# A new order of all steps in a grouped-query attention kernel, with the first bfloat16 transfers placed among GpSimd's products

## The chip, the core and the metric

The kernel runs on one core of a Trainium2 chip. The time is device microseconds of one execution. The kernel before took 352.64 us (median of three runs, 352.6 to 353.29). The engines are named as in the profile: PE (TensorE, matmul), PEld (its weight load), DVE (VectorE), ACT (ScalarE), POOL (GpSimd), SP (SyncE, which here only issues transfers).

## What is computed

Softmax attention with 8 query heads and 2 key/value heads per batch, 8 batches, 1024 positions, head dimension 64. There are 64 heads in all, numbered over batches; heads 0 to 3 use the first k and v of batch 0, heads 4 to 7 the second, and so on.

```python
batch, n_q_heads, n_kv_heads, seq, head_dim = (8, 8, 2, 1024, 64)
scores = scale * np.matmul(q_group, k_group.transpose(0, 1, 3, 2))
scores_max = np.max(scores, axis=-1, keepdims=True)
attn = np.exp(scores - scores_max)
attn = attn / (np.sum(attn, axis=-1, keepdims=True) + 1e-08)
output[:, q_start:q_end, :, :] = np.matmul(attn, v_group)
```

## The kernel before

**Tiles.** One head has 8 score tiles. A tile is 128 key positions by 1024 query positions (two matmuls, L400) in one of three PSUM slots (`sp0` to `sp2`). A slot is free again when its tile has been read by ACT or DVE. 366 of the 512 tiles go to ACT, which exponentiates them in one instruction (L411, into `pt`). The other 146 go to DVE, which computes an approximate exponential by bit arithmetic, in these steps: L422 scales the scores into 16-bit integers (`ye`), reading PSUM; L431 takes their mantissa into `zz`; `zz` is multiplied by `ye`, partly on DVE (L457), partly on POOL (L448); L463 masks `ye` in place to its exponent. The weight of such a tile is the sum of `ye` and `zz`, so PE multiplies both by v; for the last three heads DVE adds them first (L474). L431, L463 and the products work on a chain of one or two tiles (1024 or 2048 columns), as `LENGTHS` says. The mask of a chain has to wait for every product of it, since it overwrites `ye`.

**Second product.** PE multiplies the weights by v, with a column of ones that gives the sum of the weights (L491; L529 for head 0 and the last head, whose products are made tile by tile). An output piece is 128 query positions by 65 columns. Seven pieces share a PSUM bank; then DVE takes the reciprocals (L560) and normalises (L571) into `ost`, and SP stores a head at a time (L378).

**Transfers.** q, k and v are float32 in HBM. A transfer on POOL's queue casts them to bfloat16 in a scratch tensor in HBM (`qd`, `kd`, `vd`; L174): one head or two heads of q, one or two k or v of a batch. SP then brings them in: q and k through transposing transfers (L243 into `qt`, L233 into `kt`, which L237 and L238 copy to the other half of the partitions), v by plain ones (L226 into `va`). POOL is one queue: a product behind a transfer waits for the transfer's descriptors to be written.

**Order.** Nothing is scheduled by the compiler. A string, `ORDER`, holds one letter for each step, in one sequence for all engines, and a loop in the kernel issues the steps as it reads them; each engine keeps its own part of that sequence. `A0` are the scores of the next tile for ACT in slot 0, `a` to `g` those of a tile for DVE (of the current head, the next, and so on), `x` an exponential, `p` L422, `z` L431, `G2,78` a product on POOL of 8 x 78 columns of the chain two before the newest, `m` the rest of the product on DVE, `t` the mask, `+` the sum, `V` up to four matmuls of the second product, `E` and `L` those of the first and the last head, `F` a dummy matmul, `r` and `n` reciprocal and normalisation, `S` a store, `T`, `K`, `C`, `U` the transfers on SP (q, k, k's copy, v), and `q`, `k`, `v`, `X`, `Y`, `Z` those on POOL. The capital three wait besides for the last scores matmul issued before them in the sequence:

```python
if now and gate:
    tc.add_manual_dep(ins.ins, now.ins.name, Sync, reason="loads in time, not sooner")
```

A product on POOL waits for the DVE step ahead of the last of DVE's steps that work from SBUF to SBUF:

```python
tc.add_manual_dep(gps.ins, gate.ins.name, Sync, reason="the port goes to the step behind it")
```

`ORDER` begins behind a fixed head of the program: loads of the first q, k and v, their casts and transposes on PE, and the transfers of q for heads 1 and 2.

Of the kernel before, what the change touches and what calls it, by code (L numbers as in the profile page):

```python
# [606 lines left out]
```

## Time and profile before

| | before |
|---|---|
| median of three runs | 352.64 us |
| the profiled execution | 352.72 us |
| its span, first to last instruction | 350.9 us |
| mean granted clock of PE | 0.995 |
| exponentials on ACT (L411) | 366 |
| L422 on DVE | 146 |
| products on POOL (L448) | 126 |

The profiled execution is one of its own; its span leaves out 352.72 - 350.9 = 1.82 us around the instructions. A row of a timeline gives start and duration in us, the engine, the line of the kernel, the operation, output and input, and in brackets the idle time of the engine ahead of it with what ended it. A row that groups instructions gives their count, total busy time, the mean of one in ns, and the idle time ahead of them.

### The profile page before, as it was taken

To read this page: it belongs to the slowest core of one execution; us is meant where nothing else is said; L and a number is where in the kernel's file an instruction comes from. 1 tells how busy PE (TensorE), PEld (TensorE's weight loads), DVE (VectorE), ACT (ScalarE), POOL (GpSimd) and SP (SyncE) were. 2 spreads that over 40 slices of the span, in tenths; PEclk is the share of its full clock that TensorE was granted. 3 is DMA by queue.
4 is the path that set the end of the run, shared out by engine and by line. 5 is a ranking of instruction groups with operands and counts; after the bars stand their busy time and mean duration, and the time that the engine had idled before them with its cause. 6 is when DMAs were issued, how large, how long until landed. Compare 5 with 4: busy or idle time off the path is not lost.

```text
span 350.9 us, 14187 instructions
## 1 busy us (share of the span) xinstructions
PE 340.2 (97%) x6268; PEld 225.7 (64%) x6268; DVE 342.1 (97%) x518; ACT 339.8 (97%) x370; POOL 288.6 (82%) x236
## 2 busy tenths in 40 slices
PE   7879999999999999999999999999999999999995
PEld 3446665666676666666666666666665666667774
DVE  5999999999999999999999999999999999999996
ACT  5997999999999999999999999999999999999994
POOL 3496989999988999998999989899998989987000
PEclk9998999999999999999999999999999999999999
DMA  5879577865978778666768976678778765533123
GB/s 150 123 151 178 108 152 138 137 135 95 149 147 116 154 151 131 118 131 138 147 122 112 151 156 133 119 136 158 122 136 138 116 148 98 113 83 86 48 84 102
DMA packets 96606, 44.84 MB, mean 128 GB/s; under 512 B 61184, under 2 KB 95360, under 8 KB 95744
## 3 DMA queue, kind: packets, MB, share of 16 engines
q1 hardware_dynamic: 94128, 31.34, 42.3%
q0 software_dynamic: 2128, 12.19, 24.9%
q8 instruction: 49, 0.80, 1.0%
q10 hardware_dynamic: 288, 0.39, 0.3%
q14 instruction: 13, 0.11, 0.2%
HBM read 27.13 MB, written 28.97 MB: 160 GB/s over the span
## 4 chain that ended last, share of the span: by engine, by line
PE 55%; DVE 30%; ACT 8%; issue 3%; DMA 2%; SPq 0%; DVEq 0%
PE ops L491 30%; PE sp L400 24%; DVE ye L422 15%; ACT pt L411 8%; DVE ye L463 4%; DVE zz L431 4%; DVE ost L571 3%; DVE zz L457 3%; DMA kt<-kd 2%; DVE rec L560 1%; PE ops L269 1%; PE sp L529 1%; PE sp L292 0%; DVE kt L313 0%; PE ops L304 0%
## 5 line engine op out<-in xcount | busy, mean ns | idle before, releaser
L411 ACT ACTIVATE pt<-sp 128x1024 bf16<-128x1024 f32 x366 | 337.3, 1052 | 3.4 <-PE sp L400 3.2
L448 POOL TENSOR_TENSOR zz<-ye,zz 128x568 bf16<-128x568 bf16 (+29 forms) x126 | 248.5, 1973 | 25.4 <-DVE zz L431 9.0
L422 DVE TENSOR_SCALAR ye<-sp 128x1024 uint16<-128x1024 f32 x146 | 177.1, 1213 | 1.3 <-PE sp L400 0.8
L400 PE MATMUL sp<-qt,kt 64*128 64x512 bf16 x1024 | 166.5, 383 | 4.3 <-ACT pt L411 3.0
L491 PE MATMUL ops<-va,pt 128*128 128x65 bf16 x2832 | 160.6, 194 | 0.0
L491 PEld LDWEIGHTS <-pt 128*128 128x128 bf16 x2832 | 120.5, 98 | 30.7 <-issue 30.7
L491 PE MATMUL ops<-va,zz 128*128 128x65 bf16 x1136 | 123.8, 194 | 0.0
L491 PE MATMUL ops<-va,ye 128*128 128x65 bf16 x1104 | 119.6, 194 | 1.3 <-DVE ye L463 1.3
L491 PEld LDWEIGHTS <-ye 128*128 128x128 bf16 x1104 | 83.9, 98 | 16.9 <-issue 14.8
L491 PEld LDWEIGHTS <-zz 128*128 128x128 bf16 x1136 | 86.5, 98 | 9.8 <-issue 9.5
L400 PEld LDWEIGHTS <-kt 64*128 64x128 bf16 x1024 | 51.6, 93 | 58.9 <-issue 34.9
L463 DVE TENSOR_SCALAR ye<-ye 128x2048 uint16<-128x2048 uint16 (+1 forms) x77 | 51.6, 676 | 0.0
L431 DVE TENSOR_SCALAR zz<-ye 128x2048 uint16<-128x2048 uint16 (+1 forms) x77 | 49.7, 657 | 0.1
L571 DVE TENSOR_TENSOR ost<-ops,rec 128x448 f32<-128x448 f32 (+2 forms) x73 | 44.4, 608 | 0.3
L457 DVE TENSOR_TENSOR zz<-ye,zz 128x2048 bf16<-128x2048 bf16 (+31 forms) x54 | 33.4, 622 | 0.0
L174 POOL DMA_DIRECT2D qd<-in_q_dram x34 | 23.7, 697 | 5.6 <-PE sp L400 4.6
L560 DVE RECIPROCAL rec<-ops 128x7 f32<-128x7 f32 (+2 forms) x73 | 14.1, 194 | 0.0
L443 POOL MEMSET tick<- 128x1 bf16 x52 | 9.7, 187 | 0.0
L174 POOL DMA_DIRECT2D vd<-in_v_dram x8 | 5.9, 735 | 0.0
L174 POOL DMA_DIRECT2D kd<-in_k_dram x8 | 5.7, 712 | 0.0
L269 PE MATMUL ops<-warm 128*128 128x512 bf16 (+1 forms) x12 | 3.5, 448 | 1.2 <-DVE warm L168 1.2
L529 PEld LDWEIGHTS <-pt 128*128 128x128 bf16 x96 | 3.4, 98 | 1.2 <-issue 1.2
(37 smaller groups left out, 27.2 us busy)
## 6 DMA issues: line engine op xcount, KB each, us to landing
out_dram<-ost SPq DMA_DIRECT2D x63, 256.0 KB, 3.2
qd<-in_q_dram POOLq DMA_DIRECT2D x28, 256.0 KB, 4.7
kt<-kt SPq DMA_DIRECT2D x30, 64.0 KB, 3.7
va<-vd SPq DMA_DIRECT2D x30, 64.0 KB, 3.2
kd<-in_k_dram POOLq DMA_DIRECT2D x7, 256.0 KB, 4.8
vd<-in_v_dram POOLq DMA_DIRECT2D x7, 256.0 KB, 5.3
qt<-qd SPq DMA_TRANSPOSE x63, 4.2
qd<-in_q_dram POOLq DMA_DIRECT2D x7, 128.0 KB, 3.3
```

The lines of the kernel that those rows point to most:

```text
L174: return nc.gpsimd.dma_start(out=t.rearrange("(a x) d -> a (x d)", a=128), in_=src.rearrange("(a x) d -> a (x d)", a=128),)
L400: now = nc.tensor.matmul(sps[x][:, hf, :], lhsT=t[lo : lo + D, c // NH, ci % NH * 128 : (ci % NH + 1) * 128], rhs=qt[j][lo : lo + D, 0, :] ...
L411: exps.append(nc.scalar.activation(out=p, in_=where_s[(j, c)], func=AF.Exp, scale=scale))
L422: vec = nc.vector.tensor_scalar(out=ye[:, i, :, :], in0=where_s[(j, c)], scalar1=EXP_A, scalar2=EXP_B, op0=ALU.mult, op1=ALU.add,)
L431: vec = nc.vector.tensor_scalar(out=ch.tiles(zz), in0=ch.tiles(ye), scalar1=0x7F, scalar2=0x3F00, op0=ALU.bitwise_and, op1=ALU.bitwise_or,)
L443: tock = nc.gpsimd.memset(tick, 0.0) if any(old) else None
L448: gps = nc.gpsimd.tensor_tensor(out=z, in0=flat(ch.tiles(ye))[:, ch.cols : ch.cols + w], in1=z, op=ALU.mult)
L457: vec = nc.vector.tensor_tensor(out=z, in0=flat(ch.tiles(ye))[:, 0 : ch.cols], in1=z, op=ALU.mult)
L463: vec = nc.vector.tensor_scalar(out=ch.tiles(ye), in0=ch.tiles(ye), scalar1=0x7F80, scalar2=None, op0=ALU.bitwise_and,)
L491: ended[job] = nc.tensor.matmul(ops[g % 2][:, lo : lo + D + 1], lhsT=p[:, par, qs * 128 : (qs + 1) * 128], rhs=va[(b * G + h // HPG) % NVA ...
L560: vec = nc.vector.reciprocal(out=to, in_=sums)
L571: vec = nc.vector.tensor_tensor(out=to, in0=src, in1=by, op=ALU.mult)
```

## The change

Two tables change and no code: `ORDER` is another sequence throughout, and `LENGTHS` has 76 chains instead of 77 (70 of two tiles and 6 of one; before 69 and 8). Its first and last lines and the lengths:

```diff
 ORDER = """
-A0IX3TY1a1xA2pxA0za1xKA2pX4E0E2TxFA0m0E3xA1za2t1E5FxpFA0E1xm0A1E6X5zxb2t1A0pE7E4xTA1rzxb2nG0,78A0pxX
-6A1Y2m1xb2A0G0,50pxA1Tt1Z1xA2zb0VVVt1VxVVG0,78VpA1VVxVVVVrA2zc0TG1,101xnVVCpA1SVVxVVVVX8VKA2rm1A0xG0
...
+A0IX3TY1a1xA2pxA0za1xA2TpX4E0E2xFA0m0E3xb1KzA2pE5FxFFA0E6m0xFA1b2zE7X5xpFA0xA1t2Tb2zE1pxG0,56A0xt2b1
+X6A2m1E4xG0,72pA0xA2rnb1Y2t1xA0zVTVVVpVxVG0,170VA2VVVxVVrCnb0A1pTVVxSVA2VVVVm0xVX8VVVt1A0b1t0Z1xA2rV
...
-SVt0VVL1,1+1L3,1L4,1xL5,1+0L6,1L0,1rnL2,1L7,1Srn
+0+0L3,0L4,0xnL5,0L0,0rL1,0nSL6,0L7,0Srn
 """
 LENGTHS = """
-11112121222222222222222222222222222222222222222222222222222222222222222222211
+1111222222222222222222222222222222222222222222222222222222222222222222222211
 """
```

Counted over the whole sequence: 366 exponentials, 146 L422, 146 tiles in chains, 74 reciprocals and normalisations and all transfers are as many as before. L431 and L463 are 76 each instead of 77, L457 58 instead of 54, products on POOL 120 instead of 126 with 100256 columns in all instead of 99344, dummy matmuls `F` 6 instead of 3.

On POOL, from the transfer for heads 6 and 7 on (`qd` is q, `kd_0` both k and `vd_0` both v of batch 1, `vd_1` the v of heads 4 to 7), there stood before:

```order
L174 DMA qd_356<-in_q_dram 16x8192
L174 DMA kd_0_361<-in_k_dram 16x8192
L448 TENSOR_TENSOR zz<-ye,zz 128x400
L174 DMA vd_1_382<-in_v_dram 16x4096
L448 TENSOR_TENSOR zz<-ye,zz 128x624
L448 TENSOR_TENSOR zz<-ye,zz 128x808
L174 DMA qd_491<-in_q_dram 16x8192
L448 TENSOR_TENSOR zz<-ye,zz 128x248
L174 DMA vd_0_522<-in_v_dram 16x8192
L448 TENSOR_TENSOR zz<-ye,zz 128x368
```

On POOL, at the same place of the new order, from the product ahead of that transfer on, stands:

```order
L448 TENSOR_TENSOR zz<-ye,zz 128x448
L174 DMA qd_343<-in_q_dram 16x8192
L448 TENSOR_TENSOR zz<-ye,zz 128x576
L174 DMA kd_0_383<-in_k_dram 16x8192
L448 TENSOR_TENSOR zz<-ye,zz 128x1360
L174 DMA qd_487<-in_q_dram 16x8192
L174 DMA vd_1_507<-in_v_dram 16x4096
L174 DMA vd_0_529<-in_v_dram 16x8192
L448 TENSOR_TENSOR zz<-ye,zz 128x1160
```

The products are fewer and longer, heads 6/7 and the second k no longer follow each other, and both v transfers stand behind that of heads 8/9, with no product among the three.

On DVE, in the stretch that goes with the last five of POOL's rows before (a chain's L422, the steps behind it, and the mask of 2048 columns), there stood:

```order
L431 TENSOR_SCALAR zz<-ye 128x1024
L571 TENSOR_TENSOR ost<-ops_206,rec 128x256
L422 TENSOR_SCALAR ye<-sp_449 128x1024
L560 RECIPROCAL rec<-ops_393 128x7
L457 TENSOR_TENSOR zz<-ye,zz 128x616
L571 TENSOR_TENSOR ost<-ops_393,rec 128x448
L463 TENSOR_SCALAR ye<-ye 128x2048
L422 TENSOR_SCALAR ye<-sp_518 128x1024
```

On DVE, the new order has there, from head 0's first normalisation to the L431 that goes with POOL's 1160 columns:

```order
L571 TENSOR_TENSOR ost<-ops_205,rec 128x256
L463 TENSOR_SCALAR ye<-ye 128x1024
L431 TENSOR_SCALAR zz<-ye 128x2048
L422 TENSOR_SCALAR ye<-sp_380 128x1024
L560 RECIPROCAL rec<-ops_206 128x4
L571 TENSOR_TENSOR ost<-ops_206,rec 128x256
L422 TENSOR_SCALAR ye<-sp_445 128x1024
L457 TENSOR_TENSOR zz<-ye,zz 128x688
L463 TENSOR_SCALAR ye<-ye 128x1024
L463 TENSOR_SCALAR ye<-ye 128x2048
L560 RECIPROCAL rec<-ops_392 128x7
L431 TENSOR_SCALAR zz<-ye 128x2048
```

Between an L431 and the next step from SBUF to SBUF there now stand two L422 with a reciprocal and a normalisation, and the mask of 2048 columns follows its product step after one short mask. Behind this piece come L422, a normalisation of 448 columns, L422 and L457.

On SP, the transfers that bring in the q of heads 6 and 7 (`qd_356`, `qd_343`), k's copies, and v of heads 4 to 7 (`va_94`) stood before:

```order
L243 DMA_TRANSPOSE qt<-qd_356 128x1x512
L237 DMA kt<-kt 64x512
L238 DMA kt<-kt 64x512
L378 DMA out_dram<-ost 128x512
L233 DMA_TRANSPOSE kt<-kd_0_361 128x1x512
L226 DMA va_94<-vd_1_382 128x4x64 x2
```

On SP, the new order has:

```order
L237 DMA kt<-kt 64x512
L238 DMA kt<-kt 64x512
L243 DMA_TRANSPOSE qt<-qd_343 128x1x512
L378 DMA out_dram<-ost 128x512
L243 DMA_TRANSPOSE qt<-qd_343 128x1x512
L226 DMA va_94<-vd_1_507 128x4x64 x2
L233 DMA_TRANSPOSE kt<-kd_0_383 128x1x512
```

Both heads' q now come ahead of that v, and the third k behind it.

More of the change, by code (lines that the diff above doesn't have):

```diff
@@ L66 @@
[L66 to L68 removed]
+A0IX3TY1a1xA2pxA0za1xA2TpX4E0E2xFA0m0E3xb1KzA2pE5FxFFA0E6m0xFA1b2zE7X5xpFA0xA1t2Tb2zE1pxG0,56A0xt2b1
+X6A2m1E4xG0,72pA0xA2rnb1Y2t1xA0zVTVVVpVxVG0,170VA2VVVxVVrCnb0A1pTVVxSVA2VVVVm0xVX8VVVt1A0b1t0Z1xA2rV
+zVVVv1VVxVVpVA0TVG0,145VxVVVA2nb1VxUVpA0VVVVxVVKA2m0q10A1VzxVVVVVVVt1Vc0xG0,191A2rpVVVVVxVVVTA1nc0xA
@@ new lines @@
+2pSVVVVxVVVVm0q12A1c0zxA2pVG0,64VVVxVVVVA1rt1c0xVA2G0,192pVVVxVVVTA1nc0xA2pSVVVVVxVVVA1rzc0xA2pVG0,5
+6VVVCVxVVA1t1d0xVG0,184pA2TVVVxA1nc0xpA2STVVVVVxVUVVVVm0q14zA1c0xrA2pG0,63VVVVVVxVVVA1t1c0xVG0,106Vp
+A2VVVxVA1nA0xzVk2VSVVVVVVzVc2xA1G2,78rKpVVVVVxVVVVVA0m2G1,105nc2xA1pVSVVVVVxVVVVA0t2Tq16d2xA1zVVVVG2
+,78pVVxVVVVTA0VVxVrVm2VA1G1,106nc2xVVpA0SVVVxVVVA1m1A2TxVVVt2VVVVVVVt1xc0A1G0,78pVVVVxVVVVVA2rzc0xA1
+TG1,178VpVVVVCVxVVVVA2nc0xA1pVSVVVVVxVVVVA2q18rt1d0xA1KpG0,93VVVVVxVVUVVA2nA0xVzv2VVVVVVzxe1A2G2,80T
@@ new lines @@
+pVVVVxVVVA0rm2d1xA2G1,73pVVVVVxVVVA0t2e1xA2G1,183pVVVVVxVVVA0Tnd1xVVpVSA2VVxVVA0rq20t1A1VxVVzVVVVVVG
+1,106nxd2A0pVSVVVxVVVVVA1ze2xA0G2,71pTVVVVVxVVVVA1m2A2rxt2VVVVVVG1,111Vnd0xUA1pSVVVVVxVVVVTA2ze0xA1G
+2,78pVVVVVxVVVVA2rzq22e0xA1pVVG3,47VVCVxVVKVVA2m3G2,114nd0xA1pSVVVVVxVVVA2rt3e0xVVG2,106pA1TVVVxVVVV
+A2ne0xVm2VG1,71SVpA1VVxVVVA2t2k3e0xA1pVG1,54VVVVxVVVrA2m1e0xA1G0,106pTVVVVxVVVA2nA0xVzVq24VSVVVVt2d1
+xA2G1,71pVVVVxVVVVVA0ze1xA2G2,71pVVVVVVxVVVVA0m2re1t2xA2G1,191pVTVVVVVxUVVVA0nd1xA2pSVVVVVxVVVVA0rze
@@ new lines @@
+1xA2G2,65pTVVVVCVxVVVA0q26zA1xVt3VVVVVG2,114nd2xA0pVVVVxVVVKVA1rzA2v3xA0zVVVVVVxVm4VVVVVVVG3,106ne1x
+A2pVTSVVVVVxVVVVA0t4d1xA2G3,71pVVVVVVxVVVA0m3e1G2,247rxVpVVTA2VxVVA0nd1VxpVVSA2VVVxVVrVnA0A1xVm2Sq28
+t3VVVVVVt2xd2A0TG1,71pVVxVVVVA1zd2xA0G2,78pVVVVVxVVVVVA1rm2d2xA0G1,71pVVVVVVxVUVVA1t2e2xVG1,106VpVA0
+VVxVVVVTnA1A2CxzVq30VSVVVVVzVd0xA1G3,79pVVVVVxVVKVVVA2rne0G2,100xA1pVSVVVVVxVVVA2t3e0xG2,78A1pTVVVVV
+xVVVA2rm2k4A0xzVVVVVVt3Vxd1A2G2,197pVVVVxVVVVA0ne1xA2pSVVTVVVxVVA0rm1A1q32xVVVVVTVVVG2,30nVxVVVm2A2S
@@ new lines @@
+t1d0xVVG0,78VpA1VVxVVVA2rt2e0xA1G0,71pVVVVVxVVVVA2Tzd0xA1G1,107pVVVVVxVUVVVA2nA0xzVVVVVVVVt2Vxe1KA2G
+1,191rpVVVVxVVVVA0ne1CxA2pSVVVVxVVVVTA0m1q34A1zxVVVVVv4t2VVxe2A0rpG1,177VVVVxVVVA1ne2xA0pSVVVVVxVVVA
+1ze2xA0G2,79pVVVVxVVVA1rzA2xVVG2,30VnVVVVVt3q36xSe0A1pVVG2,47VxVVVVVA2Tze0xA1G3,78pVVVVVVxVVVVA2rm3A
+0xVG2,30VnVVTVVVVt3e1xSUA2G2,71pVVVVVxVVVVA0zd1xA2G3,71pVVVVVxVVVA0zd1xA2G4,71pVVVVVxVVVA0m4q38rA1t4
+xVVVKTzVVCVVxe2G4,114nA0VpVVSVxVVVA1VrxVm4VVVA2TG3,106ne0xA1pVSVVVVxVVVA2t4e0xA1G3,79pVVVVVxVVVA2rm3
@@ new lines @@
+k5A0xzVVVVVVt4Vd1xA2G3,227pTVVVVVxVVVVA0ne1xA2rpSVVVVVxVVVA0nA1xVm1q40VVVVVVxe2A0m3G2,78pVVVVxVVVVA1
+rt3e2xA0G2,178VpVVVVxVVUVVA1nd2xA0pVSVVVVVxVVVVA1t1e2xA0G0,71pTVVVVVVxVVVVt2A1e2xG0,84A0rpTVVVVVxVVV
+VA1zq42A2xVVm1VVVCVVG0,115nd0xA1pVSVVVVxVVKVVA2rzA0v5xVVVzVVVVVVxVt3VVVA1G2,106nd2xA0pTSVVVVVxVVVVzA
+1d2xm3A0G2,71pTVVVVVxVVVVA1t3e2xA0G2,121pVVVVVxVVVA1rnA2xVVVVzVSq44VVVVxe0m3A1G2,190rpVVVVVxVVVTVA2n
+d0xA1pSVVVVVVxVVVVA2t3e0xA1G2,66pVVVVVVxVVVzA2e0xG2,114rA1pVVVVVxVUVVTA2nA0xVt3VVSVVVVVq46m2VxVVVVVz
```

64 lines of the change are left out of this document (19 added, 45 removed).

## The prediction

> **What bounds the kernel now.** I read the page's busy shares first, then the timeline of ACT (which exponentials start late), then the other engines' timelines at the place where ACT stands still.
>
> ```profile
> PE 340.2 (97%) x6268; PEld 225.7 (64%) x6268; DVE 342.1 (97%) x518; ACT 339.8 (97%) x370; POOL 288.6 (82%) x236
> L411 ACT ACTIVATE pt<-sp 128x1024 bf16<-128x1024 f32 x366 | 337.3, 1052 | 3.4 <-PE sp L400 3.2
> ```
>
> Three engines show 97%, so the shares alone decide nothing. The second row does: 366 exponentials take 337.3 us together, 337.3/366 = 0.92 us from one to the next (1052 ns is one alone; neighbours overlap). Both orders have 366, so this sum is a floor.
>
> ```profile
> 6.27 19.36 ACT L411 ACTIVATE pt<-sp 128x1024 bf16<-128x1024 f32 x21 [0.45 <-PE sp L400]
> 27.22 1.94 ACT L411 ACTIVATE pt<-sp 128x1024 bf16<-128x1024 f32 x2 [1.59 <-PE sp L400]
> 30.13 28.59 ACT L411 ACTIVATE pt<-sp 128x1024 bf16<-128x1024 f32 x31 [0.97 <-PE sp L400]
> 58.88 1.94 ACT L411 ACTIVATE pt<-sp 128x1024 bf16<-128x1024 f32 x2 [0.16 <-ACT pt L411]
> ...
> 302.96 3.81 ACT L411 ACTIVATE pt<-sp 128x1024 bf16<-128x1024 f32 x4 [0.18 <-PE sp L400]
> ...
> 335.17 11.28 ACT L411 ACTIVATE pt<-sp 128x1024 bf16<-128x1024 f32 x12
> ```
>
> The brackets hold the idle time ahead of a row. After its first exponential ACT starts late by 1.59 + 0.97 + 0.16 + 0.18 = 2.90 us in all, and the sum closes: 6.27 + 337.3 + 2.90 = 346.47, while the last row ends at 335.17 + 11.28 = 346.45. Behind it stand 350.9 - 346.45 = 4.45 us of tail in the span, and 352.72 - 350.9 = 1.82 us outside it. So 2.56 of the 2.90 us sit between 25.6 and 30.1 us. What happened there, on DVE, POOL and PE:
>
> ```profile
> 22.79 0.62 DVE L571 TENSOR_TENSOR ost<-ops,rec 128x448 f32<-128x448 f32 x1
> 23.33 2.33 DVE L463 TENSOR_SCALAR ye<-ye 128x2048 uint16<-128x2048 uint16 x1
> ```
> ```profile
> 23.03 0.66 POOL L448 TENSOR_TENSOR zz<-ye,zz 128x248 bf16<-128x248 bf16 x1
> 23.64 0.55 POOL L174 DMA_DIRECT2D vd<-in_v_dram  x1
> 24.20 0.89 POOL L448 TENSOR_TENSOR zz<-ye,zz 128x368 bf16<-128x368 bf16 x1
> ```
> ```profile
> 25.71 0.20 PE L491 MATMUL ops<-va,ye 128*128 128x65 bf16 x1 [1.31 <-DVE ye L463]
> ...
> 29.62 0.90 PE L400 MATMUL sp<-qt,kt 64*128 64x512 bf16 x6
> ```
> ```profile
> L463 DVE TENSOR_SCALAR ye<-ye 128x2048 uint16<-128x2048 uint16 x69 | 48.2, 704 | 0.0
> ```
>
> The mask (L463) takes 0.70 us as a mean of 69, and 2.33 here. POOL runs product, transfer, product without a gap from 23.03 to 24.20 + 0.89 = 25.09, and the mask ends at 25.66, 0.57 behind that: it was held back for about 2.33 - 0.70 = 1.6 us. PE's second product reads that mask, so PE waits 1.31, its scores come late, and ACT waits 1.59. The second wait follows from PE's clock:
>
> ```profile
> 23.00:24.00 1.00, 0.67 (x10) 0.27 (x7) 1.00 (x2) 1.00 (x2) 0.98 (x3) 1.00 1.93 277
> 24.00:25.00 1.00, 0.41 (x4) 0.11 (x2) 1.00 (x1) 1.00 (x2) 0.98 (x2) 1.00 0.49 85
> 25.00:26.00 1.00, 0.29 (x10) 0.29 (x10) 1.00 (x2) 0.63 (x1) 0.75 (x2) 1.00 0.10 33
> ...
> 28.00:29.00 1.00, 1.00 (x21) 1.00 (x20) 1.00 (x2) 1.00 (x2) 0.79 (x1) 0.50 2.53 301
> ```
>
> In these windows of 1 us PE's busy time is the first figure behind the comma and its granted clock the third from the end. After 0.67, 0.41 and 0.29 us of work the clock stood at 0.50, and the scores of 29.62 came 0.97 late for ACT. The Trainium skill, TensorE: Matmul & The Clock Gate, What's actually happening, lets the clock fall after an idle window of about 3.4 us; here it fell with no pause above 1.31, so the trace differs, and the sum uses the trace's 0.97.
>
> **The change part by part.** (1) *The transfers among the first products.* I walk the new order with rows. Exponential n starts at 6.27 + 0.92 (n - 1). The first double mantissa step (L431 on 2048 columns, the third row of the new DVE piece above) stands behind the 14th exponential in both orders, and in the trace at 18.34:
>
> ```profile
> 18.34 0.68 DVE L431 TENSOR_SCALAR zz<-ye 128x2048 uint16<-128x2048 uint16 x1
> ...
> 19.28 1.21 DVE L422 TENSOR_SCALAR ye<-sp 128x1024 uint16<-128x1024 f32 x1
> 20.41 0.17 DVE L560 RECIPROCAL rec<-ops 128x4 f32<-128x4 f32 x1
> 20.53 0.43 DVE L431 TENSOR_SCALAR zz<-ye 128x1024 uint16<-128x1024 uint16 x1
> 20.87 0.42 DVE L571 TENSOR_TENSOR ost<-ops,rec 128x256 f32<-128x256 f32 x1
> 21.20 1.21 DVE L422 TENSOR_SCALAR ye<-sp 128x1024 uint16<-128x1024 f32 x1
> ```
> ```profile
> 18.12 1.00 POOL L174 DMA_DIRECT2D vd<-in_v_dram  x1
> ```
> ```profile
> L448 POOL TENSOR_TENSOR zz<-ye,zz 128x1336 bf16<-128x1336 bf16 x1 | 2.7, 2737 | 0.0
> L448 POOL TENSOR_TENSOR zz<-ye,zz 128x1184 bf16<-128x1184 bf16 x1 | 2.8, 2805 | 0.1
> ```
>
> From start to start L422 costs DVE 1.13, the reciprocal 0.12, L431 on 1024 columns 0.34, the short normalisation 0.33; the long one 23.33 - 22.79 = 0.54. The step ends at 19.0. POOL's 1360 columns (nearest row 1336: 2.74) run to 21.8. Until its own product step DVE has L422, reciprocal, normalisation, L422, 1.13 + 0.12 + 0.33 + 1.13 = 2.7: both meet within 0.1. Then POOL issues heads 8/9 (0.55), the v of heads 4 to 7 (not before about 22.8: it waits for scores that wait for exponential 17, over at 6.27 + 17 x 0.92 = 21.9) and batch 1's v, to about 24.0; DVE does a product step, two masks and L431 beside them, also to about 24.0. In the rows such a meeting costs the transfer, not DVE: 1.00 instead of 0.55, and L431 its usual 0.68. Then 1160 columns (row 1184: 2.8) last to 26.8, against L422, normalisation, L422 = 2.8. So no mask stands behind product, transfer, product again; I take -1.59 on ACT. Bounds: -1.59, and 0 if one block stays.
>
> (2) *The clock.* With the mask on time PE loses the stretch of 0.67, 0.41, 0.29, so I take -0.97; bounds -0.97 and 0. The order also puts 32 of head 0's matmuls later, into the thin stretch around exponentials 9 to 12, and adds three dummies of 266 ns (row below) in PE's idle time; without that cover they cost 0.8.
>
> (3) *Bookkeeping.* One L431 and one L463 fewer, four L457 more, six products fewer on POOL, which takes 912 columns more.
>
> ```profile
> L457 DVE TENSOR_TENSOR zz<-ye,zz 128x2048 bf16<-128x2048 bf16 x9 | 10.8, 1214 | 0.0
> ...
> L457 DVE TENSOR_TENSOR zz<-ye,zz 128x1024 bf16<-128x1024 bf16 x5 | 3.4, 683 | 0.0
> ...
> L269 PE MATMUL ops<-warm 128*128 128x128 bf16 x6 | 1.0, 266 | 0.0
> ```
>
> A column of L457 costs (1214 - 683)/1024 = 0.52 ns and a step 683 - 531 = 152 ns besides. DVE: -912 x 0.52 = -0.47 us, +4 x 0.15 = +0.61, and the two steps fewer at most 2 x 0.70: between -1.3 and +0.1, beside ACT. Taken: 0.
>
> (4) *The rest of the order* is new too, with the same work. ACT lost 0.16 + 0.18 = 0.34 us there; I keep 0.34. Bounds: 0, and 2.90 if a block like the first turns up once.
>
> (5) *The tail.* DVE now has the normalisation of head 61's last group (0.54) between the final sums and the last two groups, and SP two stores there instead of one.
>
> ```profile
> 346.24 0.56 DVE L571 TENSOR_TENSOR ost<-ops,rec 128x384 f32<-128x384 f32 x1
> 346.96 0.21 DVE L560 RECIPROCAL rec<-sp 128x8 f32<-128x8 f32 x1 [0.16 <-PE sp L529]
> ```
>
> DVE waited 0.16 for PE here, and one of the two sums now stands ahead of the last exponential's product, so I take 0. Bounds: 0, and 0.54 - 0.16 = +0.4 if that cover is gone.
>
> **Sum:** 352.72 - 1.59 - 0.97 = 350.16, forecast 350.2 us. The profiled execution is 0.08 above the median of 352.64, so the sum needs no correction.
>
> **The rivals.** *A, half of it comes back.* Two thin covers in the new order. First, the dense stretch on DVE from exponential 9 to 15 (three L422, four short masks or L431, one L431 on 2048, one product step, a reciprocal and a normalisation: 3.4 + 1.4 + 0.6 + 0.6 + 0.1 + 0.3 = 6.4 us) against 6 x 0.92 = 5.5 of ACT: up to 0.9 late. Second, v of heads 4 to 7:
>
> ```profile
> vd<-in_v_dram POOLq DMA_DIRECT2D x1, 128.0 KB, 4.4
> ```
> ```profile
> va<-vd SPq DMA_DIRECT2D x2, 64.0 KB, 6.8
> ```
>
> Issued at about 22.8, it lands at 27.2; the copies into va (6.8 in the window from 24 us) land at about 34.3 to 34.6, and ACT feels it only if later than about 34.9, since head 4's product comes after exponential 30 (6.27 + 30 x 0.92 = 33.9) with one exponential in hand. Against both: the margins are small but there. Price 0.6 to 1.7: 350.8 to 351.9. The Trainium skill, SBUF — State Buffer, SBUF: two separate sides, says that GpSimd cannot write descriptors while DVE holds the shared ports; by it the two masks and the L431 would push this v back by their 1.8 us, and the time would lie at this rival's upper end. The row of 1.00 agrees in kind, at 0.45 us.
>
> *B, no gain.* The blocks only move: a mask or product step elsewhere is caught once behind POOL, at 1.6 to 2.56. For it: over 100 products placed anew, and covers of 0.1 us in my walk. Against it: the old order had one such block behind 126 products. 352.0 to 353.3.
>
> *C, slower.* The burst of heads 8/9, two v transfers and 1160 columns acts as a whole as product, transfer, product did at 23.03: if DVE's product step at 21.8 is still waiting when the first transfer starts, it and the masks stay out until 0.55 x 3 + 2.8 = 4.4 us later, and the clock falls again (0.97). 350.2 + 4.4 + 0.97 - 0.9 (one exponential in hand) = 354.7. It decides the sign once the hold exceeds 2.56 + 0.7 + 0.9 = 4.2 us, all of the burst. Against it: the v of heads 4 to 7 has to wait for PE, which opens a gap.
>
> **How the numbers follow.** A measurement of this kernel tells about 0.2% (0.7 us) from no change. Forecast as walked (349.7 to 350.8) 0.50, A 0.22, B 0.16, C and other stalls of its size 0.12. Faster by more than 0.7 is forecast and A: 0.72; same 0.16; slower 0.12. The low end is 352.72 - 2.90 = 349.8, less 0.2 of scatter; the high end takes in A and two thirds of B, 352.7.
>
> **What would show it.** Right: ACT's row runs from 6.27 to about 60 without a bracket above 0.3; no L463 above 0.9 us; the clock is 1.00 from 20 to 35 us; the last exponential ends near 343.9. Step 1 is wrong if a DVE step stretches beside two products and a transfer; A shows as PE waiting for va or ACT waiting for PE near 21 or 35 us; step 4 is wrong if ACT waits more than 0.34 behind 60 us; step 5 if the tail exceeds 4.45.

## The result and the profile after

| | before | after |
|---|---|---|
| median | 352.62 us (6 executions, 352.30 to 353.29) | 349.66 us (6 executions, 349.15 to 350.35) |
| profiled execution, its span | 352.72, 350.9 us | 349.65, 347.9 us |
| ratio, 95% interval | | 0.9916, 0.9902 to 0.9931 |

The changed kernel is faster by 0.84% of the time, 3.0 us. The forecast was 350.2; the range of 349.6 to 352.7 holds the median at its low end. Measured once more, beside other kernels, it took 350.01 against 352.75: 0.9924, 0.9904 to 0.9944. A few executions, of the kernel before and of the changed one alike, ran 1.6 to 1.8% longer at a lower granted clock, and no median or ratio here counts them.

Busy shares of the page and the group of the exponentials, after:

```profile
span 347.9 us, 14191 instructions
PE 339.3 (98%) x6271; PEld 225.9 (65%) x6271; DVE 339.6 (98%) x520; ACT 339.4 (98%) x370; POOL 287.4 (83%) x228
L411 ACT ACTIVATE pt<-sp 128x1024 bf16<-128x1024 f32 x366 | 336.8, 1043 | 0.8 <-PE sp L400 0.8
```

ACT's timeline after, the exponentials alone:

```profile
6.05 29.57 ACT L411 ACTIVATE pt<-sp 128x1024 bf16<-128x1024 f32 x32 [0.34 <-PE sp L400]
35.82 4.69 ACT L411 ACTIVATE pt<-sp 128x1024 bf16<-128x1024 f32 x5 [0.20 <-PE sp L400]
40.73 302.56 ACT L411 ACTIVATE pt<-sp 128x1024 bf16<-128x1024 f32 x329 [0.22 <-PE sp L400]
```

Three rows are the whole program: ACT waits 0.20 and 0.22 after its first exponential, and never behind 41 us. The last exponential ends at 40.73 + 302.56 = 343.29, where the prediction named 343.9. With that the time splits as the prediction split it:

| term, us | before | after | forecast | measured |
|---|---|---|---|---|
| first exponential starts | 6.27 | 6.05 | 0 | -0.22 |
| 366 exponentials | 337.3 | 336.8 | 0 | -0.5 |
| ACT waits between them | 2.90 | 0.42 | -2.56 | -2.48 |
| tail in the span | 4.45 | 4.61 | 0 | +0.16 |
| outside the span | 1.82 | 1.75 | 0 | -0.07 |

The measured terms add to -3.11, the two executions differ by 3.07. The first and the last two terms scatter from one execution to the next (in the second profile of the changed kernel the first exponential starts at 6.45).

DVE's and POOL's timelines after, where the mask had been held:

```profile
21.69 0.55 DVE L457 TENSOR_TENSOR zz<-ye,zz 128x688 bf16<-128x688 bf16 x1
22.16 1.01 DVE L463 TENSOR_SCALAR ye<-ye 128x1024 uint16<-128x1024 uint16 x2
23.09 0.19 DVE L560 RECIPROCAL rec<-ops 128x7 f32<-128x7 f32 x1
23.21 0.64 DVE L431 TENSOR_SCALAR zz<-ye 128x2048 uint16<-128x2048 uint16 x1
```
```profile
19.08 2.77 POOL L448 TENSOR_TENSOR zz<-ye,zz 128x1360 bf16<-128x1360 bf16 x1
21.78 0.55 POOL L174 DMA_DIRECT2D qd<-in_q_dram  x1
23.08 1.34 POOL L174 DMA_DIRECT2D vd<-in_v_dram  x2 [0.75 <-PE sp L400]
24.43 2.40 POOL L448 TENSOR_TENSOR zz<-ye,zz 128x1160 bf16<-128x1160 bf16 x1
```

The meeting came as walked: the product ends at 21.85, DVE's product step starts at 21.69, and the two masks and L431 run while POOL has only transfers. The row of two L463 holds a mask of 1024 columns and one of 2048, 0.42 and 0.68 each; L431 takes 0.64. No L463 of this profile takes more than 0.89. The windows of 1 us show PE full and the clock at 1.00, where before it had 0.67, 0.41 and 0.29 of work:

```profile
23.00:24.00 1.00, 1.00 (x29) 0.91 (x27) 1.00 (x4) 1.00 (x2) 0.92 (x2) 1.00 2.10 265
24.00:25.00 1.00, 1.00 (x19) 0.63 (x19) 1.00 (x2) 1.00 (x2) 0.98 (x2) 1.00 0.09 16
25.00:26.00 1.00, 1.00 (x13) 0.46 (x11) 1.00 (x2) 1.00 (x2) 1.00 (x1) 1.00 1.16 289
```

### The profile page after: what moved, and what is told of

It is laid out like the page before. It is cut to its first block, busy times and chain, and to the rows that moved or that the text cites. A ratio compares the mean times of both kernels' runs of the same rounds, so it can differ in the third digit from the quotient of the medians.

```text
span 347.9 us, 14191 instructions
## 1 busy us (share of the span) xinstructions
PE 339.3 (98%) x6271; PEld 225.9 (65%) x6271; DVE 339.6 (98%) x520; ACT 339.4 (98%) x370; POOL 287.4 (83%) x228
## 4 chain that ended last, share of the span: by engine, by line
PE 65%; DVE 11%; issue 1%; DVEq 0%
PE ops L491 36%; PE sp L400 28%; DVE ye L422 6%; DVE ye L463 2%; DVE ost L571 1%; DVE zz L431 1%; DVE zz L457 1%; PE sp L529 1%; DVE rec L560 0%; DVEq L602 0%; DVEq L463 0%
## 5 line engine op out<-in xcount | busy, mean ns | idle before, releaser
L411 ACT ACTIVATE pt<-sp 128x1024 bf16<-128x1024 f32 x366 | 336.8, 1043 | 0.8 <-PE sp L400 0.8
L448 POOL TENSOR_TENSOR zz<-ye,zz 128x848 bf16<-128x848 bf16 (+26 forms) x120 | 248.2, 2069 | 22.1 <-DVE zz L431 8.9
L422 DVE TENSOR_SCALAR ye<-sp 128x1024 uint16<-128x1024 f32 x146 | 177.7, 1217 | 0.7 <-PE sp L400 0.5
L400 PE MATMUL sp<-qt,kt 64*128 64x512 bf16 x1024 | 166.3, 382 | 3.2 <-ACT pt L411 2.0
L491 PE MATMUL ops<-va,zz 128*128 128x65 bf16 x1136 | 126.0, 194 | 0.0
L491 PE MATMUL ops<-va,ye 128*128 128x65 bf16 x1104 | 121.8, 194 | 0.0
L400 PEld LDWEIGHTS <-kt 64*128 64x128 bf16 x1024 | 52.2, 93 | 57.4 <-issue 34.2
L463 DVE TENSOR_SCALAR ye<-ye 128x2048 uint16<-128x2048 uint16 (+1 forms) x76 | 49.8, 662 | 0.0
L431 DVE TENSOR_SCALAR zz<-ye 128x2048 uint16<-128x2048 uint16 (+1 forms) x76 | 49.6, 662 | 0.0
L457 DVE TENSOR_TENSOR zz<-ye,zz 128x2048 bf16<-128x2048 bf16 (+29 forms) x58 | 33.6, 583 | 0.0
L174 POOL DMA_DIRECT2D qd<-in_q_dram x34 | 22.3, 656 | 4.9 <-PE sp L400 4.1
L443 POOL MEMSET tick<- 128x1 bf16 x50 | 11.6, 232 | 0.0
L269 PE MATMUL ops<-warm 128*128 128x128 bf16 (+1 forms) x15 | 4.0, 402 | 1.2 <-DVE warm L168 1.2
(37 smaller groups left out, 27.2 us busy)
```

What stands on the lines that cost most here:

```text
L174: return nc.gpsimd.dma_start(out=t.rearrange("(a x) d -> a (x d)", a=128), in_=src.rearrange("(a x) d -> a (x d)", a=128),)
L400: now = nc.tensor.matmul(sps[x][:, hf, :], lhsT=t[lo : lo + D, c // NH, ci % NH * 128 : (ci % NH + 1) * 128], rhs=qt[j][lo : lo + D, 0, :] ...
L411: exps.append(nc.scalar.activation(out=p, in_=where_s[(j, c)], func=AF.Exp, scale=scale))
L422: vec = nc.vector.tensor_scalar(out=ye[:, i, :, :], in0=where_s[(j, c)], scalar1=EXP_A, scalar2=EXP_B, op0=ALU.mult, op1=ALU.add,)
L431: vec = nc.vector.tensor_scalar(out=ch.tiles(zz), in0=ch.tiles(ye), scalar1=0x7F, scalar2=0x3F00, op0=ALU.bitwise_and, op1=ALU.bitwise_or,)
L443: tock = nc.gpsimd.memset(tick, 0.0) if any(old) else None
```

## Experiments: what held the mask

Theory: POOL's products, run without a gap, kept DVE's mask out, and that stall with the fall of the clock behind it was worth 2.56 us. Rival: the stall belongs to the order of the work around it. The first three kernels are the kernel before with one letter group moved or gone. The fences show the piece of `ORDER` around an edit, without its line breaks; `v1` is batch 1's v transfer. A ratio is against the kernel before in the same session, whose median there was 352.46 (e1 to e4), 352.63 (e5 to e7), 352.75 (e8 and e9) or 352.12 (e10 and e11).

**e1.** Batch 1's v transfer ahead of the 248-column product:

```diff
-VVVVX8VKA2rm1A0xG0,31nVVb1t1v1UxA2pVG0,46
+VVVVX8v1VKA2rm1A0xG0,31nVVb1t1UxA2pVG0,46
```

> The kernel before with one step moved: the transfer of batch 1's v is issued ahead of GpSimd's 248-column product instead of between it and the 368-column product. Theory (the mask at 23.33 us was held back by product, transfer, product without a gap on GpSimd): the double mask there takes 0.7 to 0.9 us instead of 2.33, PE's wait of 1.31 and ScalarE's waits of 1.59 and 0.97 go, and the time falls to 350.0 to 350.4 us. Rival (the stall comes of the order of the head's and PE's work around it, which is unchanged here): ScalarE waits about 1.6 near 26 us as before and the time stays within 352.3 to 353.

Measured: 350.39 us against 352.46, 0.9946 (0.9916 to 0.9975). The profiled execution was one of the two of ten that took about 351.95. In it DVE came a microsecond later, and the mask met the two products, now next to each other; POOL and DVE:

```profile
23.59 0.49 POOL L174 DMA_DIRECT2D vd<-in_v_dram  x1
24.10 1.50 POOL L448 TENSOR_TENSOR zz<-ye,zz 128x248 bf16<-128x248 bf16 x2
```
```profile
24.44 1.71 DVE L463 TENSOR_SCALAR ye<-ye 128x2048 uint16<-128x2048 uint16 x1
```

The time speaks for the theory. The profile does not show it: the mask, begun 0.34 behind the first product's start, took 1.71 instead of the expected 0.7 to 0.9 and ended at 26.15, 0.55 behind the end of the second product (25.60). No profile of one of the eight faster executions was taken; e7 and e11 below show the same move with the mask on time.

**e2.** The transfer behind both products:

```diff
-nVVb1t1v1UxA2pVG0,46VV
+nVVb1t1UxA2pVG0,46v1VV
```

> The kernel before with the same transfer moved behind the 368-column product: the two products (248 and 368 columns, 0.66 and 0.89 us) stand next to each other on GpSimd. Theory one, the transfer between the products keeps DVE out as the products do: the mask is held back by the two products alone, ends about 0.55 earlier than 25.66, at 25.1, the second wait shrinks with the first, and the time is about 351.9 or less. Theory two, DVE gets in between two products that stand next to each other, and only the transfer in between closed the gap: the mask ends at about 24.4, the stall is gone and the time is 350.0 to 350.4. Rival (neither matters): 352.3 to 353.

Measured: 351.48, 0.9993 (0.9961 to 1.0024). POOL and DVE:

```profile
23.09 1.50 POOL L448 TENSOR_TENSOR zz<-ye,zz 128x248 bf16<-128x248 bf16 x2
24.53 0.71 POOL L174 DMA_DIRECT2D vd<-in_v_dram  x1
```
```profile
23.38 1.77 DVE L463 TENSOR_SCALAR ye<-ye 128x2048 uint16<-128x2048 uint16 x1
```

Theory one, by the mask: it ended at 25.15, 0.56 behind the second product (24.59), and DVE did not get in between two products. The time decides nothing, since the interval includes no change.

**e3.** The 368-column product gone, its columns on DVE:

```diff
-xA2pVG0,46VVVVx
+xA2pVVVVVx
```

> The kernel before without the 368-column product on GpSimd; DVE does those columns itself (about 0.2 us more in its own product step). What is left at 23 us is one product of 0.66 and the transfer of 0.55. If the second product is needed for the hold, the mask ends at about 24.4 and the time is 350.0 to 350.5. If the transfer alone keeps DVE out behind the product, the mask ends at about 24.8 and some 0.3 to 0.8 of ScalarE's first wait stays: 350.6 to 351.3. Rival: unchanged, 352.3 to 353.

Measured: 351.72, 1.0003 (0.9972 to 1.0035); eight executions from 350.35 to 354.45. POOL, DVE, PE and ACT:

```profile
23.10 0.67 POOL L448 TENSOR_TENSOR zz<-ye,zz 128x248 bf16<-128x248 bf16 x1
23.70 0.72 POOL L174 DMA_DIRECT2D vd<-in_v_dram  x1
```
```profile
23.39 0.94 DVE L463 TENSOR_SCALAR ye<-ye 128x2048 uint16<-128x2048 uint16 x1
```
```profile
36.77 0.61 PE L400 MATMUL sp<-qt,kt 64*128 64x512 bf16 x4 [1.61 <-DMA qt<-qd]
```
```profile
37.41 1.02 ACT L411 ACTIVATE pt<-sp 128x1024 bf16<-128x1024 f32 x1 [1.19 <-PE sp L400]
```

The mask ended at 24.33, 0.56 behind the product and well inside the transfer: with no product behind it the transfer does not keep DVE out; DVE costs the transfer 0.17 (0.72 for 0.55), and the transfer ends 0.09 behind the mask. So the second product is what made the stall long. But the time did not fall clearly (the interval reaches from 1.0 us less to 1.2 more), although ACT's wait near 26 us was gone. In its place stands a wait that the trace of before had not shown: PE stood 1.61 us for a transposed q, and ACT 1.19 behind it. The expectation missed this, and the next section but one is on it.

## Experiments: the clock

**e4.** Twenty dummies inside the stall:

```diff
-v1UxA2pVG0,46
+v1UxA2pFFFFFFFFFFFFFFFFFFFFVG0,46
```

> The kernel before with 20 matmuls on the warm-up tile added on PE inside the stall, just ahead of the head's first matmul that waits for the late mask. Nothing else is changed. Theory (the second wait of 0.97 comes of the clock of 0.50 that follows PE's thin stretch): the mask still takes 2.33 and ScalarE still waits about 1.6 once, but the clock stays at 1.00 from 27 to 30 us, the wait of 0.97 goes, and the time is about 351.7. Rival (the second wait has another cause, such as the late mask's own successors): both waits stay, 352.3 to 353. Third: the dummies themselves delay PE by more than the stall covers, and the time is over 353.

Measured: 351.91, 0.9990 (0.9969 to 1.0011). The mask still took 2.34 (23.36 to 25.70). Windows, and ACT's rows:

```profile
24.00:25.00 1.00, 1.00 (x17) 0.83 (x16) 1.00 (x1) 1.00 (x2) 0.98 (x2) 1.00 1.47 304
...
27.00:28.00 1.00, 1.00 (x23) 0.58 (x20) 1.00 (x3) 1.00 (x2) 0.19 (x1) 1.00 0.71 150
```
```profile
27.00 10.40 ACT L411 ACTIVATE pt<-sp 128x1024 bf16<-128x1024 f32 x11 [1.36 <-PE sp L400]
37.79 1.02 ACT L411 ACTIVATE pt<-sp 128x1024 bf16<-128x1024 f32 x1 [0.39 <-PE sp L400]
39.01 23.28 ACT L411 ACTIVATE pt<-sp 128x1024 bf16<-128x1024 f32 x25 [0.20 <-PE sp L400]
```

The clock stayed at 1.00 and the wait of 0.97 at 30 us went, as the theory says, and 0.39 + 0.20 of it came back at 37.8, again for a transposed q. So the interval includes no change, and what the clock is worth in time is read from the trace alone.

In the profile of e1 the clock fell earlier, at 18 us. Its windows:

```profile
16.00:17.00 1.00, 0.66 (x4) 0.19 (x4) 1.00 (x3) 1.00 (x2) 1.00 (x3) 1.00 0.59 131
17.00:18.00 1.00, 0.51 (x4) 0.20 (x4) 1.00 (x2) 1.00 (x3) 0.98 (x2) 0.88 1.97 262
18.00:19.00 1.00, 1.00 (x7) 0.26 (x5) 1.00 (x3) 1.00 (x3) 1.00 (x2) 0.50 0.00 0
...
21.00:22.00 1.00, 1.00 (x20) 0.59 (x17) 0.18 (x1) 0.83 (x2) 1.00 (x1) 0.91 0.72 137
```

The kernel before has the same thin stretch at 15 to 18 us (0.47, 0.66, 0.41), and its profiled execution kept the clock there.

Why a thin stretch drops the clock in one execution and not in another can be read from the traces. In the clock records of the fourteen profiles each stretch at one clock, but for the last, which the record cuts off, is a whole number of steps of 3.413 us (1, 4, 6, 94, 96, 100 and 101). So the last fall, behind the end of PE's work, gives the grid of these steps for each profile. Count the columns of all matmuls that start in a step, those of L400 (64 rows in) by half: of the 1424 steps, the 18 ahead of a fall have 3072 or fewer, all others 3055 or more. The kernel before counts 2714 from 22.99 to 26.41, just ahead of its fall. The profile of e4 has a step at nearly the same place (22.94 to 26.36); there it counts 5209, of which 2560 are the dummies, so without them it would have 2649. So e4 does show the cause. The start of the grid differs from one execution to the next, and it decides which of the two thin stretches of the old order drops the clock. In the profile of the kernel before the thinnest stretch of that length between 8 and 45 us counts 2064, in e11 4575, and in the two of the changed kernel 3600, so that no start of the grid would drop their clock.

How often it falls can be told from the mean granted clock of each execution: it is 0.993 to 0.995 in the four profiles with a fall in the course of the kernel and 0.997 or more in the ten without. It was 0.995 or less in 63 of 74 executions of the kernel before, in 2 of 10 of e1, in 5 of 10 of e4 (which leaves the first thin stretch as it is), and in none of the 11 of the changed kernel.

**e11.** e1 with 24 dummies in that first stretch:

```diff
-A0pxX6A1Y2m1xb2A0G0,50pxA1Tt1Z1xA2zb0
+A0FFFFFFpxX6A1FFFFFFY2m1xb2A0FFFFFFG0,50pxA1FFFFFFTt1Z1xA2zb0
```

Beside this, those dummies write to columns of the PSUM bank that hold no sums.

> The kernel of e1 (before with batch 1's v transfer ahead of the 248-column product) with 24 matmuls on the warm-up tile added on PE, 6 at each of four places between 14 and 18 us, where PE is busy for 0.39 to 0.66 of each microsecond. Theory (the clock of 0.50 at 18 to 21 us in the profile of e1 follows PE's thin stretch, as it does at 27 us in the kernel before): the clock is 1.00 from 14 to 30 us, ScalarE has no wait at 20 us, the mask near 23.4 takes 0.9 or less, and no execution takes over 351.2 (of those that are not disturbed); median 350.0 to 350.6. Rival (the fall has nothing to do with how busy PE is): some executions still show a mean granted clock of 0.993 to 0.995 and take 351.9, as 2 of 10 did in e1.

Measured: 350.25, six executions from 350.00 to 350.45, 0.9948 (0.9928 to 0.9968). PE's work at 15 to 18 us is now 0.92, 1.00 and 0.98 and the clock 1.00. (e7, whose grid of steps stands at the same place, kept its clock there without dummies, so this profile alone shows nothing of them.) DVE, POOL and ACT:

```profile
23.35 0.69 DVE L463 TENSOR_SCALAR ye<-ye 128x2048 uint16<-128x2048 uint16 x1
```
```profile
23.03 0.49 POOL L174 DMA_DIRECT2D vd<-in_v_dram  x1
23.53 1.86 POOL L448 TENSOR_TENSOR zz<-ye,zz 128x248 bf16<-128x248 bf16 x2
```
```profile
6.25 50.03 ACT L411 ACTIVATE pt<-sp 128x1024 bf16<-128x1024 f32 x54 [0.38 <-PE sp L400]
56.44 243.94 ACT L411 ACTIVATE pt<-sp 128x1024 bf16<-128x1024 f32 x265 [0.16 <-ACT pt L411]
300.56 43.48 ACT L411 ACTIVATE pt<-sp 128x1024 bf16<-128x1024 f32 x47 [0.19 <-PE sp L400]
```

Here the mask came first, 0.18 ahead of the products, took its usual 0.69, and the products waited instead (1.86 together, 1.50 in e2). With mask and clock both out of the way, ACT's waits in the old order are 0.35 in all, near 56 and 300 us. No execution took over 350.45 or had a mean clock under 0.997, where e1 had two of ten near 351.95 at 0.993 and 0.994: the theory's side, on few executions.

**e8.** The changed kernel without the three dummies that it has more:

```diff
-E5FxFFA0E6m0xFA1b2zE7X5xpFA0
+E5FxFA0E6m0xA1b2zE7X5xpA0
```

> The changed kernel as it is, as the measure for the next two on the same chip. 349.2 to 350.2.

> The changed kernel without the three matmuls on the warm-up tile that it has more than the kernel before. Theory (what keeps PE's clock up between 14 and 20 us is the work of head 0 that now stands there, 0.69 to 0.91 of each microsecond at 15 to 18 us): clock 1.00 from 14 to 30 us, no further wait, time as that of the changed kernel within 0.3 us. Rival (the dummies keep the clock up): in some executions the clock falls as in the profile of e1 at 17 to 20 us, those take 1 to 1.5 us longer and their mean granted clock is 0.993 to 0.995.

Measured: the changed kernel again 350.01, without the dummies 349.57 (349.19 to 350.50), against before 0.9916 (0.9900 to 0.9931). The clock is 1.00 from 14 to 38 us in both profiles. The dummies do nothing measurable; the work that stands there, head 0's moved matmuls among it, is enough without them (PE is busy for 0.70 to 0.91 of each microsecond from 15 to 18 in this profile). In the second profile of the changed kernel ACT has no wait at all behind its first exponential:

```profile
6.45 336.73 ACT L411 ACTIVATE pt<-sp 128x1024 bf16<-128x1024 f32 x366 [0.62 <-PE sp L400]
```

## Experiments: what is late next

In e2, e3 and e4 PE waited 0.83, 1.61 and 0.81 for a transposed q until 36.60, 36.77 and 37.14. By the order it is that of head 8, whose first scores (for DVE) stand behind 32 of ACT's tiles in the old order and stop the tiles behind them. SP transposes it behind the q of head 7, which is needed 10 of ACT's tiles later. Three kernels turn the two round:

```diff
-            turn_q(tq_next)
+            turn_q({7: 8, 8: 7}.get(tq_next, tq_next))
```

> The kernel of e3 (before without the 368-column product on GpSimd) with one more change: SP transposes the queries of head 8 ahead of those of head 7, which are needed later. Theory (behind the held mask stands a second limit, head 8's queries, for which PE waited until 36.6 to 37.1 in e2, e3 and e4): the wait of 1.2 that ScalarE had near 37.4 in e3 shrinks to 0.3 or less, ScalarE's waits are about 0.5 in all and the profiled execution takes 350.2 to 350.8 with a granted clock of 1.00. Rival (PE's wait there is for something else that comes at the same time, such as the keys of batch 1): the 1.2 stays, 351.5 to 352.

> The kernel before with only the queries of head 8 transposed ahead of those of head 7. Theory (the mask's stall comes first and hides the second limit): the mask still takes 2.3, ScalarE's first wait of 1.4 to 1.6 stays, and the time falls by no more than 0.6, to 351.9 to 352.6. Rival (head 8's queries are the limit in most executions and the mask's stall is hidden by them): the time falls to 351 or less.

> The kernel of e1 (before with batch 1's v transfer ahead of the 248-column product) with the queries of head 8 transposed ahead of those of head 7. Theory (transfers do not keep DVE out, products next to each other do, and with the transfers first the mask runs beside them): the double mask near 23.3 us takes 0.9 or less, no wait at 37, and the old order with these two moves takes 349.8 to 350.3 in executions whose clock stays at 1.00 from 15 to 30 us. Rival (two products of 248 and 368 next to each other hold the mask wherever they stand, 1.7 us as in the profile of e1): ScalarE keeps a wait of 0.7 near 26 us and the time is 350.8 to 351.4. If the clock falls behind PE's thin stretch of 15 to 18 us, as in the profile of e1, both are 1.5 later.

e5 has this and no 368-column product: 351.50, 0.9976 (0.9958 to 0.9995); its profile has a fall of the clock at 18 us, and ACT's wait near 37 is 0.51 where e3 had 1.19. e6 has it alone: 352.54, 0.9996 (0.9976 to 1.0017). e7 has it with e1's move: 350.54, 0.9952 (0.9929 to 0.9975), no better than e1. In e7 DVE's mask took 0.70 from 23.60, ahead of the products at 23.79, which settles e7's first question for the theory. But PE waited still, and the view of transfers tells why. DVE's row, PE's row, SP's queue (start, and how long SP was at issuing) and the transfer (us from its issue to its landing), e7:

```profile
23.60 0.70 DVE L463 TENSOR_SCALAR ye<-ye 128x2048 uint16<-128x2048 uint16 x1
```
```profile
35.96 0.61 PE L400 MATMUL sp<-qt,kt 64*128 64x512 bf16 x4 [0.87 <-DMA qt<-qd]
```
```profile
28.27 4.85 SPq L243 DMA_TRANSPOSE qt<-qd  x2
```
```profile
qt<-qd SPq DMA_TRANSPOSE x1, 7.6
```

Head 8's q, now the first of the two, was issued at 28.27 and landed 7.6 later, at 35.8; PE goes on 0.1 behind that. In e3, as the second, it landed at 36.6, 0.3 behind the first (27.49 + 8.8 = 36.3). The two land 0.3 to 0.6 apart in these profiles, so their order buys about half a microsecond: my expectation for e5 (0.3 or less of the wait left) was wrong, and its rival too, since the wait is for q and shrank. What decides is when SP comes to the first of them, 26.6 to 28.3 in these profiles, and how long it takes to land, 6.1 to 8.8. In the profile of the kernel before SP came to it at 26.63 and both had landed by 34.6, so no wait was to be seen. In e11, with SP there at 26.77, head 8's q landed at 34.9 and PE waited 0.20. In e1's profile it landed at 35.9, and ACT had by then lost 1.64 to other waits, so it was not late. Why it lands earlier in e11 than in e2 and e3 (36.5 and 36.6) is not settled: e11 issues the v transfer 0.7 to 1.5 earlier, but so does e7, where PE waited 0.87.

The stall that e6 was expected to keep is not in its profile. This is of an execution of 350.85, and shows how the kernel before, whose executions ran from 350.8 to 353.2 in these sessions but for one of 355.9, can lose less: the clock fell at 18 us, DVE came 1.0 later, and the mask arrived 0.06 ahead of the end of the first product:

```profile
23.58 0.77 POOL L448 TENSOR_TENSOR zz<-ye,zz 128x248 bf16<-128x248 bf16 x1
24.30 0.77 POOL L174 DMA_DIRECT2D vd<-in_v_dram  x1
25.09 0.90 POOL L448 TENSOR_TENSOR zz<-ye,zz 128x368 bf16<-128x368 bf16 x1
```
```profile
24.29 0.68 DVE L463 TENSOR_SCALAR ye<-ye 128x2048 uint16<-128x2048 uint16 x1
```

The same three steps on POOL, and no stall: it got in beside the transfer. Why it got in here and not in the kernel before, where it arrived 0.36 ahead of that end, is left open. That the faster executions of the kernel before are of this kind is inferred; no profile of one was taken. Their mean clock agrees: of the 17 in these sessions that took under 351.8, 11 are at 0.995 or less, so a fall alone does not cost an execution the whole stall.

Two more kernels try to take the last waits out of the changed order.

**e9.** SP transposes batch 1's k and head 8's q ahead of the copies of v of heads 4 to 7:

```diff
-A0TVG0,145VxVVVA2nb1VxUVpA0VVVVxVVKA2
+A0TKVG0,145VxVVVA2nb1VxTUVpA0VVVVxVVA2
...
-G0,191A2rpVVVVVxVVVTA1nc0x
+G0,191A2rpVVVVVxVVVA1nc0x
```

> The changed kernel with two steps of SP's queue moved: the transposes of batch 1's keys and of head 8's queries stand ahead of the copies of v of heads 4 to 7, which wait for their transfer until 29.95 us. Theory (PE's wait of 0.41 at 39.7 is for head 8's queries, queued behind those copies): head 8's queries land by about 34 instead of 39.6, the waits of 0.41 on PE and 0.22 on ScalarE go, ScalarE keeps only the 0.20 near 35.6, and the time is 0.2 lower than the changed kernel's. Rival (the transposes take the transfer engines from the copies of v, which then land later): the wait near 35.6 grows from 0.20 to 0.5 or more and the time is the same or higher.

**e10.** POOL issues v of heads 4 to 7 ahead of the q of heads 8 and 9:

```diff
-VX8VVVt1A0b1t0Z1xA2r
+VZ1X8VVVt1A0b1t0xA2r
```

> The changed kernel with the transfer of v of heads 4 to 7 issued ahead of the one for the queries of heads 8 and 9, right behind GpSimd's 1360-column product. Theory (ScalarE's wait near 35.6 to 36.5, 0.20 in the changed kernel and 0.48 in e9, is for the copies of that v, which wait for its transfer): the v is issued about 0.7 to 1.3 us earlier, the copies into va on SP's queue start by about 28.5 instead of 29.95, and no wait stands between 35 and 37 us; time 349.0 to 349.8. Rival (the margin is taken up by the spread of the transfers from one execution to the next): waits of 0 to 1.4 between 29 and 41 us as in the three profiles of the changed kernel and its variants, time 349.2 to 350.4.

e9: 350.41, 0.9935 (0.9917 to 0.9953); e10: 349.64, 0.9933 (0.9907 to 0.9959). Neither can be told from the changed kernel. In e9 head 8's q landed at 27.21 + 7.8 = 35.0 (33.68 + 5.9 = 39.6 in the changed kernel's first profile), and PE's wait of 0.41 at 39.7 is gone, as the theory says. (The profile puts this wait down to a mask that ended at 39.66; but PE started 0.14 behind the landing, as it did for q in e2, e3, e4, e7 and e11.) But the copies of v, now behind it, took 6.2 and landed at 35.2 and 35.7 (34.3 and 35.0 there), and ACT's wait near 36 grew, as the rival says. In the other three profiles of this order both copies landed by 34.4, and ACT has no wait near 36. ACT in e9:

```profile
36.52 307.15 ACT L411 ACTIVATE pt<-sp 128x1024 bf16<-128x1024 f32 x334 [0.48 <-PE sp L400]
```

In e10 the copies of v start at 26.35 and no wait stands from 35 to 37, but another, larger, stands ahead of it, as in e8: PE's rows of e8 and of e10.

```profile
29.54 0.60 PE L400 MATMUL sp<-qt,kt 64*128 64x512 bf16 x4 [1.80 <-DMA qt<-qd]
```
```profile
29.87 0.60 PE L400 MATMUL sp<-qt,kt 64*128 64x512 bf16 x4 [1.53 <-DMA qt<-qd]
```

This is the q of head 6. It is the same transpose with the same neighbours on its queue; SP's rows and the time to landing in the changed kernel and in e8:

```profile
20.09 2.53 SPq L243 DMA_TRANSPOSE qt<-qd  x1
```
```profile
qt<-qd SPq DMA_TRANSPOSE x1, 6.9
```
```profile
20.04 4.02 SPq L243 DMA_TRANSPOSE qt<-qd  x1
```
```profile
qt<-qd SPq DMA_TRANSPOSE x1, 9.5
```

Landing at 27.0 it costs nothing, at 29.5 it costs ACT 1.35. That is what is left in the changed order: waits of 0 to 1.5 us between 29 and 41 us that depend on how long a transpose takes in an execution (0.42, 0, 1.52, 0.48 and 1.27 in the five profiles of the order and its variants).

## Why the prediction was right, step by step

**Step 1, the transfers among the first products (-1.59): right in place, and the mechanism needs one word changed.** The mask was held by POOL, not by the order around it: e1, e7 and e11, which leave the work of DVE and PE in that place as it is, gain 1.9 to 2.1 us. But the transfer is not what held it: a mask that comes while a transfer runs takes its usual 0.69 or 0.70 (e7, e11). A mask that arrives well within a product ends 0.55 to 0.57 behind the last of the products (before, e1, e2, e3), two products held it and one held it only to its end; a mask that comes first goes first (e7, e11). The Trainium skill, SBUF — State Buffer, SBUF: two separate sides, has the first to start keep the shared ports for its whole instruction; e11 and e2 agree with that, and e2 adds that of two products in a row the second goes ahead of a waiting mask. Its other sentence, which the prediction drew on for rival A, that descriptors can't be written while DVE holds the ports, agrees too: a transfer beside a mask took 0.72 and 0.77 instead of 0.55 and ended 0.09 and 0.10 behind the mask (e3, e6). In the fourteen profiles 413 transfers took POOL over 0.64 us, and 399 of them ended 0.09 to 0.10 behind an L463 or L431; the other 14, one in each program, are its first. The price is small here because such a DVE step lasts 0.7 us or less.

**Step 2, the clock (-0.97): right, and for the reason given.** In the profile of e4 the dummies, and nothing else, kept the clock up, and that wait went. The working named two things for the thin stretch of the new order, head 0's matmuls and three dummies; the dummies are not needed (e8). And I saw only one of the two thin stretches as a price in the old order: at 15 to 18 us the clock fell in the profiles of e1, e5 and e6. The trace disagrees with the rule of the Trainium skill, TensorE: Matmul & The Clock Gate, What's actually happening, as the prediction quoted it (an idle window ahead of a fall), if idle means that PE does nothing: PE was busy for 0.52 to 0.61 of the step ahead of these falls. The free-running window of about 3.4 us in the same section of the Trainium skill agrees with the steps of 3.413 us found above. It can be read from the windows of 1 us too: a window's share at half clock is twice what its granted clock lacks to 1.00, so e1 has 0.24 + 3 + 0.18 = 3.42 us.

**The two are not a sum on their own, and that is the step that was missing.** Where a stall goes, something else is late next: I named the v of heads 4 to 7, and not the q of head 8 in the old order. Taking the second product away (e3) removed the stall and the fall of the clock, 2.56 of waits, and ACT waited 1.62 in other places. The changed order gets the whole, most likely because its first scores of head 8 stand behind 37 of ACT's tiles instead of 32: 5 x 0.92 = 4.6 us later (this was not tried by itself). So that -2.56 came out nearly whole (-2.48) is luck in part: it had a help that the working did not contain.

**Step 3, bookkeeping (0): nothing contradicts it.** DVE is busy 339.6 instead of 342.1; 1.6 of this is the mask's own wait, the remaining -0.9 lies inside the range of -1.3 to +0.1.

**Step 4, the rest of the order (0, with 0.34 kept): right in the size of its waits, wrong in their place, and with a gain that the working did not have.** The two old waits near 58 and 303 us went, which I had kept; 0.42 came near 36 and 41 us instead. Besides, the 366 exponentials themselves took 336.8 and not 337.3, which I had called a floor. It is 336.7 to 336.9 in all five profiles of the new order and 337.3 to 337.7 in the nine of the old, so it belongs to the order. Restarts are little of it: an exponential that starts after a wait costs 1.02 and not 0.92 (a row of one in e4), and e11, with two restarts like the changed kernel, still has 337.4. What shortens the mean of one from 1047 to 1052 ns to 1043 was not tried.

**Step 5, the tail (0): +0.16, within 0 to +0.4, and not by the mechanism feared.** By the sign that the prediction named for it, a tail over 4.45, the step would count as wrong (4.61). But the cover held: DVE's normalisation there ends at 343.44, ahead of its wait for PE's last sums, which is 0.38 instead of 0.16. From the last exponential to the last normalisation it is 1.53 us (1.50 before); the rest is stores landing, and scatters (tail 5.02 in the second profile).

**Rivals.** A had the right weak spot: the v of heads 4 to 7 was issued at 23.08 and landed 6.9 later, at 30.0, not at 27.2, but its copies took 4.4 and 4.6 and not 6.8, so they landed at 34.4 and 35.0, near the 34.3 to 34.6 that came of two terms wrong in opposite directions (27.2 + 6.8 is 34.0; the working did not say what the rest was for). If ACT's wait near 36 is theirs, as e9 and the landings of the five profiles suggest, the price was 0.20 here and 0.48 there, under the 0.6 I had named. DVE did hold up the issue of that v, but only by an L431: it took 0.86 instead of 0.55, since it began when the masks were nearly over. The first cover, the dense stretch on DVE, cost nothing. B and C did not happen: no L463 of 2048 columns exceeds 0.9 and none waits behind the transfers.

In short: of the 2.7 to 3.0 us, 1.9 is the held mask with the clock of both thin stretches (e11 against before: 352.12 - 350.25), and the remaining 0.8 to 1.1 is the rest of the order: by the profiles of e11 and of the changed kernel 0.6 to 0.7 in the exponentials, whose cause is open, and the later waits, 0.35 there against 0 and 0.42 here.

## What to carry to other kernels

When a stall is taken away, walk every queue for the next arrival within the time you mean to gain, transposes and their landing above all; a wait that the stall hides is in no bracket of the trace. Where DVE and GpSimd share a stretch, ask which of the two arrives first and whether a second product stands right behind; a transfer in that place costs little. And look at several executions: one profile shows one of the places where the clock can fall, and one of the landings that a transfer can have. The mean granted clock of each execution tells how often it falls.
